# Feed-forward up-projections as seven Strassen block products, in groups of three row tiles, in a hybrid encoder block

## The chip, the cores and the metric

The kernel runs on one core of a Trainium2 chip. The time is device microseconds of one execution of the whole block; the profile is one execution recorded by the hardware profiler. PE is the matrix engine, PEld its weight load, DVE the vector engine, ACT the scalar engine, POOL GpSimd, and SP the engine that issues most DMAs.

## The reference

One layer of an encoder block for a sequence of 1024 with 1024 channels, in float32:

```python
h = rms_norm(x, norm_mix_g)
proj = h @ w_in                               # MLA, RWKV-7 and gate columns
o_a = mla_branch(...)                         # latent attention, 8 heads
o_b = rwkv7_branch(...)                       # forward and backward recurrence
x = x + (sig(gA) * (o_a @ w_o[:512]) + sig(gB) * (o_b @ w_o[512:])) @ w_merge
h = rms_norm(x, norm_ffn_g)
gp = dwconv_centered(h @ w_ffn_gate, ffn_conv_w, ffn_conv_b)   # three taps along the sequence
x = x + (silu(gp) * (h @ w_ffn_up)) @ w_ffn_down               # hidden width 2816
```

## The kernel before

Everything is held transposed: channels on the partitions, the 1024 positions along the free axis, so that a product makes one row tile of 128 output channels by 1024 positions, as two halves of 512 (`HT`), each in its own PSUM bank.

**Products.** A float32 operand is carried as the sum of two fp32r tiles, and a product is three passes: weight high part by operand high and low part, weight low part by operand high part (`mmk`, lines 248, 249 and 251). A step of 128 rows of depth is six matmuls of 128x512. The operands in x are split once and stay in SBUF; each weight block of 128x512 (four steps) is loaded by a DMA of SP's, and `split` (lines 163 and 164) makes its parts: ACT copies the high part (`whi`), POOL subtracts it (`wlo`). `product` runs the steps of a whole row tile.

**Phases.** A and B are the projection, the attention and the recurrence; the order of PE's instructions there is worked out by the kernel's own generators. Phase C makes the branches' second part, the merge (`w_merge`, eight row tiles into `x2`) and, after each row tile of the merge, the feed-forward part's operand: `h2h` and `h2l` (the residual times the norm's gain, split) in the places of `hp`, a pool on the right side of SBUF. The sum of squares for 1/rms gathers in `acc`; `rs2` (1/rms) multiplies the products when they leave PSUM.

**Phase D** is the feed-forward part. It goes over 22 row tiles f of the hidden width, in four groups (6, 6, 5, 5). For each f the gate product (8 steps) and the up product (8 steps) use 96 matmuls. The gate product leaves PSUM as `u` (L1517), is convolved (ACT L1522, DVE L1523 and L1524), goes through Silu (L121) and times rs2 (POOL, L1527), then is multiplied by the up product (L1528), and the result is split into `sh` and `sl`. After a group, eight down products over its tiles are added to `x2` (L1535); after the last group each row tile of x2 is stored.

**Order.** PE's instructions run in the order in which the code emits them (`manual_schedule`), each engine's queue in order. The order of DVE, ACT, POOL and SP is set by the framework's scheduler, from its own estimates. PSUM in phase D is four double banks in turn (`big4`).

Of the kernel before, what the change touches and what calls it, by code (L numbers as in the profile page):

```python
# [10 lines left out]
F32 = mybir.dt.float32  # L11
R = mybir.dt.float32r
# [17 lines left out]
GROUPS = ((0, 6), (6, 12), (12, 17), (17, 22))  # L30
# [18 lines left out]
# How long a step of phase B takes to be ready after it has left TensorE's queue, in ns  # L49
# [39 lines left out]
def block_kernel(ctx: ExitStack, tc: tile.TileContext, a):  # L89
# [539 lines left out]
    def gate_done(j):  # L629
        def done(ps):  # L630
            for x, hs in zip(ps, HT):
                gt = wpool["g"].tile([128, 512], F32, tag="gt", name="gt")
                V.tensor_tensor(out=gt, in0=x, in1=rstd[:, hs], op=mult)
                (G if j >= 14 else nc.sync).dma_start(d_gate[j][:, hs], gt)
# [996 lines left out]
```

## Time and profile before

| | |
|---|---|
| time, median of 3 runs | 2131.5 us (2128.46 to 2133.38) |
| span of the profiled execution | 2126.6 us |
| time of that execution itself | not listed apart; the span lies 4.9 us below the median of the runs |
| PE busy | 1958.1 us (92%), 12280 matmuls |
| DVE, ACT, POOL busy | 997.4, 843.1, 871.8 us |
| HBM traffic | 151.20 MB read, 63.60 MB written, 101 GB/s over the span |
| phase D | from 1394 us to the end |

In the profile's rows a group or an instruction is named by its line, engine, operation and tiles (out<-in); behind it stand busy or own time and the idle time of its engine just before, with what ended that. The granted clock is that of PE, as a share of full speed.

### The profile page before, as it was taken

How to read it: one execution, taken by the hardware profiler on the slowest of the kernel's cores; microseconds unless marked ns; L12 is line 12 of the kernel's file. 1: busy time of each engine (PE TensorE's matmuls, PEld its weight loads, DVE VectorE, ACT ScalarE, POOL GpSimd, SP SyncE). 2: the span in 40 equal slices, each digit the busy share in tenths (PEclk: the TensorE clock that was granted, in tenths of full speed). 3: DMA queues.
4: the chain of work that ended last, by engine and by line, in shares of the span. 5: the costliest groups of instructions: out<-in, count | busy, mean ns of one | idle time of the engine just before them, and what ended most of it. 6: DMA issues, size and time to landing. Idle time of an engine off the chain costs nothing.

```text
span 2126.6 us, 31745 instructions
## 1 busy us (share of the span) xinstructions
PE 1958.1 (92%) x12280; PEld 1507.2 (71%) x12280; DVE 997.4 (47%) x1560; ACT 843.1 (40%) x1459; POOL 871.8 (41%) x763
## 2 busy tenths in 40 slices
PE   7799999899898779888779999999999999999999
PEld 5566667677666556556557678888888888888887
DVE  8566766626474768667773235232212321221321
ACT  4676564123233546565547644232212211221221
POOL 7344546133233646564546432433323322332331
PEclk9899999899998989999989999999999999999999
DMA  3047447354344334352433685111111111111113
GB/s 144 34 140 230 145 162 219 104 145 113 98 130 125 78 108 106 104 135 79 100 86 91 205 303 189 50 45 50 43 53 50 50 43 52 50 39 56 50 38 117
DMA packets 212551, 221.09 MB, mean 104 GB/s; under 512 B 114152, under 2 KB 138792, under 8 KB 212400
## 3 DMA queue, kind: packets, MB, share of 16 engines
q1 hardware_dynamic: 212080, 218.01, 33.4%
q8 instruction: 97, 1.59, 0.3%
q0 software_dynamic: 320, 1.05, 0.1%
q14 instruction: 54, 0.44, 0.1%
HBM read 151.20 MB, written 63.60 MB: 101 GB/s over the span
## 4 chain that ended last, share of the span: by engine, by line
PE 51%; DVE 7%; DMA 3%; issue 1%; SPq 1%; POOL 0%; ACT 0%; DVEq 0%; POOLq 0%; ACTq 0%
PE b L251 13%; PE b L248 13%; PE b L249 13%; DMA IN<-dn 2%; DVE Ti L815 2%; DVE tm L811 2%; DVE mx L1151 1%; PE po L1179 1%; PE st L1205 1%; PE po L1181 1%; PE st L1207 1%; PE po L1180 1%; PE st L1206 1%; PE ct L972 1%; PE st L248 1%
## 5 line engine op out<-in xcount | busy, mean ns | idle before, releaser
L164 POOL TENSOR_TENSOR wlo<-wraw,whi 128x512 fp32r<-128x512 f32 x248 | 306.8, 1240 | 792.6 <-ACT whi L163 788.7
L163 ACT CAST whi<-wraw 128x512 fp32r<-128x512 f32 x248 | 145.2, 586 | 652.4 <-PE b L249 462.1
L248 PE MATMUL b<-h2h,whi 128*128 128x512 f32 x704 | 274.3, 390 | 0.0
L249 PE MATMUL b<-h2l,whi 128*128 128x512 f32 x704 | 273.9, 389 | 0.0
L1217 POOL TENSOR_TENSOR pl<-pe,ph 128x512 fp32r<-128x512 f32 x128 | 169.6, 1327 | 131.2 <-ACT ph L1216 128.6
L251 PE MATMUL b<-h2h,wlo 128*128 128x512 f32 x704 | 216.7, 389 | 0.0
L248 PE MATMUL st<-hh,whi 128*128 128x512 f32 x408 | 176.0, 431 | 15.2 <-ACT hh L275 9.0
L249 PE MATMUL st<-hl,whi 128*128 128x512 f32 x408 | 164.7, 404 | 0.5 <-DVE hl L276 0.5
L248 PEld LDWEIGHTS b<-h2h,whi 128*128 128x128 f32 x704 | 132.2, 188 | 27.7 <-issue 0.2
L249 PEld LDWEIGHTS b<-h2l,whi 128*128 128x128 f32 x704 | 132.2, 188 | 27.7 <-issue 0.2
L251 PEld LDWEIGHTS b<-h2h,wlo 128*128 128x128 f32 x704 | 132.2, 188 | 27.5
L251 PE MATMUL st<-hh,wlo 128*128 128x512 f32 x408 | 140.9, 400 | 0.5 <-POOL wlo L164 0.5
L248 PE MATMUL b<-sh,whi 128*128 128x512 f32 x352 | 138.8, 394 | 0.0
L249 PE MATMUL b<-sl,whi 128*128 128x512 f32 x352 | 138.7, 394 | 0.0
L1535 DVE TENSOR_TENSOR x<-b,x 128x1024 f32<-128x1024 f32 x32 | 39.2, 1225 | 197.6 <-PE b L251 197.6
L811 DVE TENSOR_TENSOR tm<-IN,Ti 128x126 f32<-128x126 f32 (+22 forms) x248 | 91.2, 368 | 77.5 <-DMA IN<-dn 71.3
L251 PE MATMUL b<-sh,wlo 128*128 128x512 f32 x352 | 110.4, 394 | 0.0
L248 PEld LDWEIGHTS st<-hh,whi 128*128 128x128 f32 x408 | 79.6, 195 | 43.0 <-issue 9.8
L815 DVE TENSOR_TENSOR Ti<-Ti,tm 128x126 f32<-128x126 f32 (+22 forms) x248 | 104.3, 421 | 6.6
L1517 DVE TENSOR_TENSOR u<-b,rs 128x1024 f32<-128x1024 f32 x22 | 26.9, 1224 | 169.6 <-PE b L251 158.4
L1216 ACT CAST ph<-pe 128x512 fp32r<-128x512 f32 x128 | 79.1, 620 | 64.5 <-PE po L1181 61.3
L980 POOL TENSOR_TENSOR sm<-RR,pcs 64x128 f32<-64x128 f32 x112 | 47.6, 425 | 126.4 <-DVE RR L1002 105.2
(333 smaller groups left out, 4159.1 us busy)
## 6 DMA issues: line engine op xcount, KB each, us to landing
wraw<-w_in SPq DMA_DIRECT2D x64, 256.0 KB
wraw<-w_fg SPq DMA_DIRECT2D x44, 256.0 KB
wraw<-w_fu SPq DMA_DIRECT2D x44, 256.0 KB
ld<-d_x SPq DMA_DIRECT2D x32, 256.0 KB
wraw<-w_fd SPq DMA_DIRECT2D x32, 256.0 KB
d_gate<-gt SPq DMA_DIRECT2D x28, 256.0 KB
xt<-xT SPq DMA_DIRECT2D x8, 512.0 KB
d_s<-sg SPq DMA_DIRECT2D x8, 512.0 KB
```

Source lines behind the costliest of these rows:

```text
L163: S.copy(hi, x)
L164: (eng or G).tensor_tensor(out=lo, in0=x, in1=hi.bitcast(F32), op=sub)
L248: nc.tensor.matmul(o, wh, xh[:, hs], start=first, stop=False)
L249: nc.tensor.matmul(o, wh, xl[:, hs], start=False, stop=False)
L251: nc.tensor.matmul(o, wl, xh[:, hs], start=False, stop=last)
L811: t = V.tensor_tensor(out=tm[:, 0:nt, 0:nj], in0=IN[:, s, s + 1:32][:, :, None].to_broadcast([128, nt, nj]), in1=Ti[:, s, 0:nj][:, None, : ...
L815: V.tensor_tensor(out=Ti[:, s + 1:32, 0:nj], in0=Ti[:, s + 1:32, 0:nj], in1=tm[:, 0:nt, 0:nj], op=add)
L980: state["pool"] = G.tensor_tensor(out=sm[hs], in0=RR[hs, :, h, 0, :], in1=pcv[hs, i // 4, :, i % 4, None].to_broadcast([64, 2, C]), op=mult)
L1216: S.copy(ph, pe)
L1217: G.tensor_tensor(out=pl, in0=pe, in1=ph.bitcast(F32), op=sub)
L1517: V.tensor_tensor(out=u, in0=pg, in1=rs2, op=mult)
L1535: V.tensor_tensor(out=x2[:, j, :], in0=ps, in1=x2[:, j, :], op=add)
```

## The change

The two products of a tile f are one product of a 2x2 block matrix: up and gate rows of the weights (`w_fu`, `w_fg`), each in two halves of the depth (A11, A12 the up weights, A21, A22 the gate weights, 128x512 each), by the operand in two halves of the depth and two of the positions (B11, B12; B21, B22). Instead of eight block products it makes seven, by Strassen's scheme in Winograd's form, from sums of weights (s1 = A21+A22, s2 = s1-A11, A11-A21, A12-s2, on DVE) and of operand blocks (U1 to U4, made once). A block product is called a quarter and is 12 matmuls: four steps of three passes on one bank. In PE's order they are A11 by B11 (bank ba), s2 by U2 (bb), s1 by U1 (bc), A11-A21 by U3 (bb again), A12 by B21 (ba), A22 by U4 (bb), A12-s2 by B22 (bc). A bank that is used again goes on accumulating, so its next quarter waits until DVE or ACT has read what it held (p1, u2, u3, u[1]); the results are put together by DVE when they leave PSUM. So 84 matmuls a tile.

Beside that:

- The groups are eight: six of three tiles, two of two. The down products of a group are emitted after the third quarter of the next group's first tile; those of the last group at the end, the first three of them interleaved by step.
- Operand blocks: B11, U1, B21, B22 lie in hp, U2 and U3 in a new pool bq, U4 in phase D's pool fp. They are made in the merge's loop, U4 from U2 and x2 when phase D starts. An operand block is four pairs of 128x512.
- Weights: six raw tiles, three pairs of parts in turn (`parts_`). PSUM in phase D is eight single banks.
- The stores of the gate tiles 14 and 15 in phase A go from ACT's queue instead of POOL's, and the framework's scratch for dynamic DMAs is 1024 bytes.

The core of the diff (removed comments are left out):

```diff
-GROUPS = ((0, 6), (6, 12), (12, 17), (17, 22))
+GROUPS = ((0, 3), (3, 6), (6, 9), (9, 12), (12, 15), (15, 18), (18, 20), (20, 22))
...
-                (G if j >= 14 else nc.sync).dma_start(d_gate[j][:, hs], gt)
+                (S if j >= 14 else nc.sync).dma_start(d_gate[j][:, hs], gt)
...
+    def quarters(pairs):
+        return [tuple(p[k // 2][:, HT[k % 2]] for p in pairs) for k in range(4)]
+    def in_hp(i, n):
+        return quarters([[place(f"h{x}{i + q}", f"{n}{x}") for q in range(2)] for x in "hl"])
+    def in_pool(pl, n, i):
+        return quarters([[pl.tile([128, T], R, tag=f"b{i + 2 * c + q}", name=f"{n}{x}{q}") for q in range(2)] for c, x in enumerate("hl")])
+    B11, U1, B21, B22 = in_hp(0, "b11"), in_hp(2, "t1"), in_hp(4, "b21"), in_hp(6, "b22")
+    U2, U3 = in_pool(bq, "t2", 0), in_pool(bq, "t3", 4)
+    tq = y2.enter_context(pool("tq"))
     acc = place("rstd", "acc2", F32)
+    def scaled(dst, src, g):
+        S.activation(dst[0], src, AF.Copy, scale=g)
+        V.scalar_tensor_tensor(out=dst[1], in0=src, scalar=g, in1=dst[0].bitcast(F32), op0=mult, op1=sub)
     for j in range(8):
         ps, two_ = big4()
         for _ in product(two_, a["w_merge"][j], yx):
             pass
         V.tensor_tensor(out=x2[:, j, :], in0=ps, in1=x2[:, j, :], op=add)
-        h2x.append((place(f"hh{j}", "h2h"), place(f"hl{j}", "h2l")))
-        hh, hl = h2x[j]
-        S.activation(hh, x2[:, j, :], AF.Copy, scale=vc("gffn", j))
-        V.scalar_tensor_tensor(out=hl, in0=x2[:, j, :], scalar=vc("gffn", j), in1=hh.bitcast(F32), op0=mult, op1=sub)
+        k, g = j % 4, vc("gffn", j)
+        x1, x2_ = (x2[:, j, hs] for hs in HT)
+        if j < 4:
+            scaled(B11[k], x1, g)
+            d = tq.tile([128, 512], F32, tag="d", name="d")
+            G.tensor_tensor(out=d, in0=x2_, in1=x1, op=sub)
+            scaled(U1[k], d, g)
+        else:
+            g0, x10, x20 = vc("gffn", k), *(x2[:, k, hs] for hs in HT)
+            scaled(B21[k], x1, g)
+            scaled(B22[k], x2_, g)
+            d = tq.tile([128, 512], F32, tag="d", name="b12")
+            S.activation(d, x20, AF.Copy, scale=g0)
+            t3 = tq.tile([128, 512], F32, tag="t3", name="t3f")
+            V.scalar_tensor_tensor(out=t3, in0=x2_, scalar=g, in1=d, op0=mult, op1=sub)
+            split(t3, *U3[k], V)
+            t2 = tq.tile([128, 512], F32, tag="t2", name="t2f")
+            V.scalar_tensor_tensor(out=t2, in0=x10, scalar=g0, in1=t3, op0=mult, op1=add)
+            split(t2, *U2[k], V)
...
+    U4 = in_pool(fp, "t4", 0)
...
+    for k in range(4):
+        t = f5("up", 1)
+        V.scalar_tensor_tensor(out=t, in0=x2[:, 4 + k, HT[0]], scalar=vc("gffn", 4 + k), in1=U2[k][0].bitcast(F32), op0=mult, op1=sub)
+        V.tensor_tensor(out=t, in0=t, in1=U2[k][1].bitcast(F32), op=sub)
+        split(t, *U4[k], V)
+    nraw, nwt = [0], [0]
+    def raw_():
+        nraw[0] += 1
+        if nraw[0] % 6 == 0:
+            return wpool["g"].tile([128, 512], F32, tag="gt", name="ra")
+        return f5("ra", 5)
+    def parts_(x, n=512):
+        nwt[0] += 1
+        if nwt[0] % 3 == 0:
+            hi, lo = (fp.tile([128, 512], R, tag=t, name=t) for t in ("wh", "wl"))
+        else:
+            hi, lo = (wpool["w"].tile([128, 512], R, tag=t, name=t) for t in ("whi", "wlo"))
+        hi, lo = hi[:, 0:n], lo[:, 0:n]
+        split(x, hi, lo)
+        return hi, lo
+    def quarter(ps, w, xs, first):
+        for k, (xh, xl) in enumerate(xs):
+            ws = slice(k * 128, (k + 1) * 128)
+            for m, (wt, x) in enumerate(((w[0], xh), (w[0], xl), (w[1], xh))):
+                nc.tensor.matmul(ps, wt[:, ws], x, start=(first and k == 0 and m == 0), stop=(k == 3 and m == 2), skip_group_check=True)
+    sh, sl = {}, {}
+    def gate_up(f):
+        def load(w, h):
+            t = raw_()
+            nc.sync.dma_start(t, a[w][f][:, HT[h]])
+            return t
+        A11, A21, A22 = load("w_fu", 0), load("w_fg", 0), load("w_fg", 1)
+        s1, s2 = raw_(), raw_()
+        A12 = load("w_fu", 1)
+        ba, bb, bc = bank(), bank(), bank()
+        quarter(ba, parts_(A11), B11, True)
+        p1 = f5("p1")
+        S.copy(p1, ba)
+        V.tensor_tensor(out=s1, in0=A21, in1=A22, op=add)
+        V.tensor_tensor(out=s2, in0=s1, in1=A11, op=sub)
+        V.tensor_tensor(out=A21, in0=A11, in1=A21, op=sub)
+        quarter(bb, parts_(s2), U2, True)
+        u2 = f5("u2")
+        V.tensor_tensor(out=u2, in0=bb, in1=p1, op=add)
+        if f == 0:
+            for hs in HT:
+                ss = bank()
+                nc.tensor.matmul(ss, ones, acc[:, hs], start=True, stop=True)
+                rsqrt_(rs2[:, hs], ss, 1.0 / D, eps)
+        quarter(bc, parts_(s1), U1, True)
+        V.tensor_tensor(out=s2, in0=A12, in1=s2, op=sub)
+        yield
+        quarter(bb, parts_(A21), U3, False)
+        u3 = f5("u3")
+        V.tensor_tensor(out=u3, in0=bb, in1=p1, op=add)
+        quarter(ba, parts_(A12), B21, False)
+        u = fp.tile([128, T], F32, tag="u", name="u")
+        V.tensor_tensor(out=u[:, HT[1]], in0=bc, in1=u3, op=add)
+        quarter(bb, parts_(A22), U4, False)
+        V.tensor_tensor(out=u[:, HT[0]], in0=bb, in1=p1, op=add)
+        V.tensor_tensor(out=u, in0=u, in1=rs2, op=mult)
+        quarter(bc, parts_(s2), B22, False)
+        cv = fp.tile([128, T], F32, tag="cv", name="cv")
+        S.activation(cv, u, AF.Identity, scale=vc("cw1", f), bias=vc("cb", f))
+        V.scalar_tensor_tensor(out=cv[:, 1:], in0=u[:, :-1], scalar=vc("cw0", f), in1=cv[:, 1:], op0=mult, op1=add)
+        V.scalar_tensor_tensor(out=cv[:, :-1], in0=u[:, 1:], scalar=vc("cw2", f), in1=cv[:, :-1], op0=mult, op1=add)
+        act(cv, cv, AF.Silu)
+        G.tensor_tensor(out=cv, in0=cv, in1=rs2, op=mult)
+        up = f5("up")
+        V.tensor_tensor(out=cv[:, HT[0]], in0=ba, in1=cv[:, HT[0]], op=mult)
+        V.tensor_tensor(out=up, in0=bc, in1=u2, op=add)
+        V.tensor_tensor(out=cv[:, HT[1]], in0=up, in1=cv[:, HT[1]], op=mult)
+        sh[f], sl[f] = (fp.tile([128, T], R, tag=t, name=t, bufs=3) for t in ("sh", "sl"))
+        split(cv, sh[f], sl[f], V)
+        yield
+    def down(f0, f1, last):
+        n = f1 - f0
+        def weights(j):
+            t = wpool["w"].tile([128, n * 128], F32, tag="wraw", name="wraw")
+            nc.sync.dma_start(t, a["w_fd"][j, :, f0 * 128:f1 * 128])
+            return parts_(t, n * 128)
+        def mm(two_, w, k):
+            ws = slice(k * 128, (k + 1) * 128)
+            mmk(two_, w[0][:, ws], w[1][:, ws], (sh[f0 + k], sl[f0 + k]), k == 0, k == n - 1)
+        def out(j, two_):
+            for o, hs in zip(two_, HT):
+                V.tensor_tensor(out=x2[:, j, hs], in0=o, in1=x2[:, j, hs], op=add)
+            if last:
+                nc.sync.dma_start(a["outT"][j * 128:(j + 1) * 128, :], x2[:, j, :])
+        j0 = 0
+        if last:
+            j0 = 3
+            js = [([bank(), bank()], weights(j)) for j in range(3)]
+            for k in range(n):
+                for two_, w in js:
+                    mm(two_, w, k)
+            for j, (two_, _) in enumerate(js):
+                out(j, two_)
+        for j in range(j0, 8):
+            two_, w = [bank(), bank()], weights(j)
+            for k in range(n):
+                mm(two_, w, k)
+            out(j, two_)
...
     for gi, (f0, f1) in enumerate(GROUPS):
         for f in range(f0, f1):
+            part = gate_up(f)
+            next(part)
+            if f == f0 and gi:
+                down(*GROUPS[gi - 1], False)
+            next(part)
+    down(*GROUPS[-1], True)
```

How it moves instructions. DVE in phase D, one tile before (the gate product's way out of PSUM to the split result):

```order
L1517 TENSOR_TENSOR u_13872<-b_13811,rs_12751 128x1024
L1523 SCALAR_TENSOR_TENSOR cv<-u_13872,vec,cv 128x1023
L1524 SCALAR_TENSOR_TENSOR cv<-u_13872,vec,cv 128x1023
L1528 TENSOR_TENSOR sg_13939<-b_13874,sg_13939 128x1024
L164 TENSOR_TENSOR sl<-sg_13939,sh 128x1024
```

DVE after, inside a group, from the taps of one tile on (ra is a raw weight tile or a sum of two, p the copy of p1, bank a PSUM bank; u_14138 is u2 and u_14173 is u3 of the tile that follows):

```order
L1617 SCALAR_TENSOR_TENSOR cv<-u,vec,cv 128x1023
L1618 SCALAR_TENSOR_TENSOR cv<-u,vec,cv 128x1023
L1596 TENSOR_TENSOR u_14138<-bank,p_14117 128x512
L1622 TENSOR_TENSOR cv<-bank,cv 128x512
L1624 TENSOR_TENSOR cv<-up,cv 128x512
L164 TENSOR_TENSOR sl<-cv,sh 128x1024
L1591 TENSOR_TENSOR ra<-ra 128x512
L1607 TENSOR_TENSOR u_14173<-bank,p_14117 128x512
L1593 TENSOR_TENSOR ra<-ra 128x512
L1610 TENSOR_TENSOR u<-bank,u_14173 128x512
L1592 TENSOR_TENSOR ra<-ra 128x512
L1612 TENSOR_TENSOR u<-bank,p_14117 128x512
```

The additions u2 and u3 of a tile now stand between the last steps of the tile before it, and u3 stands behind that tile's sl and behind the first weight sum (L1591) of the tile after.

ACT at the step from the merge into phase D, before (the last two row tiles of the merge, each with the two weight casts of a product ahead of time, then the first function of 1/rms):

```order
L163 CAST whi<-wraw 128x512 x2
L1488 ACTIVATE h2h<-x_12750,vec 128x1024
L1493 ACTIVATE rs_12751<-x_12750 128x1024
L163 CAST whi<-wraw 128x512 x2
L121 ACTIVATE rs_12751<-b_13731,cst 128x1024
```

ACT there after (the last row tile of the merge, the high parts of its operand blocks, then the first casts of phase D):

```order
L1497 ACTIVATE b21h<-x_12750,vec 128x512
L1497 ACTIVATE b22h<-x_12750,vec 128x512
L1527 ACTIVATE rs_12751<-x_12750 128x1024
L163 CAST t3h_13138<-t3f 128x512
L163 CAST t2h_13134<-t2f 128x512
L163 CAST t4h_13746<-up 128x512
L163 CAST whi<-ra 128x512
```

The first weight casts of phase D stood two products ahead; now the first of them (whi from ra) stands behind the operand blocks of the last merge row tile and behind the first high part of U4 (t4h).

DVE at the same place after, from the last addition into x2 on (b21l, b22l, t3l, t2l are low parts, up is the temporary of U4):

```order
L1504 TENSOR_TENSOR x_12750<-b_13658,x_12750 128x1024
L1519 SCALAR_TENSOR_TENSOR t3f<-x_12750,vec,b_13724 128x512
L1498 SCALAR_TENSOR_TENSOR b21l<-x_12750,vec,b21h 128x512
L1522 SCALAR_TENSOR_TENSOR t2f<-x_12750,vec,t3f 128x512
L1498 SCALAR_TENSOR_TENSOR b22l<-x_12750,vec,b22h 128x512
L164 TENSOR_TENSOR t3l_13140<-t3f,t3h_13138 128x512
L164 TENSOR_TENSOR t2l_13136<-t2f,t2h_13134 128x512
L1546 SCALAR_TENSOR_TENSOR up<-x_12750,vec,t2h_13133 128x512
L1547 TENSOR_TENSOR up<-up,t2l_13135 128x512
L164 TENSOR_TENSOR t4l_13748<-up,t4h_13746 128x512
```

Eight operations stand between that addition and the tile from which t4h is cast.

More of the change, by code (lines that the diff above doesn't have):

```diff
@@ L1450, in block_kernel @@
     rs2 = xp2.tile([128, T], F32, name="rs2")
-    y2, tl = ExitStack(), ExitStack()
+    bq = ctx.enter_context(pool("bq"))
+    y2 = ExitStack()
     yq = y2.enter_context(pool("yq"))
     yx = [(yq.tile([128, T], R, name=f"yh{j}"), yq.tile([128, T], R, name=f"yl{j}")) for j in range(8)]
-    yp = tl.enter_context(pool("yp"))
-    psc = [ctx.enter_context(psum("psc", 2))]
+    psc = [y2.enter_context(psum("psc", 2))]
     nps = [0]
@@ L1465, in block_kernel @@
         if j == 2:
-            psc.append(ctx.enter_context(psum("psc1", 2, "right")))
-        y0 = yp.tile([128, T], F32, tag="y0", name="y0", bufs=2)
+            psc.append(y2.enter_context(psum("psc1", 2, "right")))
+        y0 = bq.tile([128, T], F32, tag=f"b{j % 2}", name="y0")
         nc.sync.dma_start(y0, d_y0[j])
-        y = yp.tile([128, T], F32, tag="gt", name="gt", bufs=2)
+        y = bq.tile([128, T], F32, tag=f"b{2 + j % 2}", name="gt")
         for _ in branch(1, j, xs, big4()[1], y):
@@ L1498, in block_kernel, with bank, f5 @@
     fp = ctx.enter_context(pool("fp"))
-    ones = fp.tile([128, 128], F32, name="ones")
-    G.memset(ones, 1.0)
-    sh = fp.tile([128, 6, T], R, name="sh")
-    sl = fp.tile([128, 6, T], R, name="sl")
-    def ft(n, tag):
-        return fp.tile([128, T], F32, tag=tag, name=n, bufs=2)
+    pd = ctx.enter_context(psum("pd", 8))
+    U4 = in_pool(fp, "t4", 0)
+    def bank():
+        return pd.tile([128, 512], F32, tag="bank", name="bank")
+    def f5(n, bufs=1):
+        return fp.tile([128, 512], F32, tag=n, name=n, bufs=bufs)
@@ L1507, in block_kernel @@
     for gi, (f0, f1) in enumerate(GROUPS):
         for f in range(f0, f1):
-            pg, two_ = big4()
-            for _ in product(two_, a["w_fg"][f], h2x):
-                pass
-            if f == 0:
-                ss = big4()[0]
-                mm32(ss, ones, acc)
-                rsqrt_(rs2, ss, 1.0 / D, eps)
-            u = ft("u2", "f2")
-            V.tensor_tensor(out=u, in0=pg, in1=rs2, op=mult)
-            pu, two_ = big4()
-            for _ in product(two_, a["w_fu"][f], h2x):
-                pass
@@ L1521, in block_kernel @@
-            cv = ft("cv", "f0")
-            S.activation(cv, u, AF.Identity, scale=vc("cw1", f), bias=vc("cb", f))
-            V.scalar_tensor_tensor(out=cv[:, 1:], in0=u[:, :-1], scalar=vc("cw0", f), in1=cv[:, 1:], op0=mult, op1=add)
-            V.scalar_tensor_tensor(out=cv[:, :-1], in0=u[:, 1:], scalar=vc("cw2", f), in1=cv[:, :-1], op0=mult, op1=add)
-            sg = ft("sg2", "f1")
-            act(sg, cv, AF.Silu)
-            G.tensor_tensor(out=sg, in0=sg, in1=rs2, op=mult)
-            V.tensor_tensor(out=sg, in0=pu, in1=sg, op=mult)
@@ L1529, in block_kernel @@
-            split(sg, sh[:, f - f0, :], sl[:, f - f0, :], V)
-        n = f1 - f0
-        for j in range(8):
-            ps, two_ = big4()
-            for _ in product(two_, a["w_fd"][j, :, f0 * 128:f1 * 128], [(sh[:, k, :], sl[:, k, :]) for k in range(n)]):
-                pass
-            V.tensor_tensor(out=x2[:, j, :], in0=ps, in1=x2[:, j, :], op=add)
-            if gi == len(GROUPS) - 1:
-                nc.sync.dma_start(a["outT"][j * 128:(j + 1) * 128, :], x2[:, j, :])
+            part = gate_up(f)
```

5 lines of the change are left out of this document (2 added, 3 removed).

## The prediction

> **What bounds the kernel now.** I read the page first, then the feed-forward stage, where the change works, in windows and by groups of instructions, and last single instructions there. The page (second block: busy tenths in 40 slices of the span):
>
> ```profile
> span 2126.6 us, 31745 instructions
> PE 1958.1 (92%) x12280; PEld 1507.2 (71%) x12280; DVE 997.4 (47%) x1560; ACT 843.1 (40%) x1459; POOL 871.8 (41%) x763
> PE   7799999899898779888779999999999999999999
> PEclk9899999899998989999989999999999999999999
> ```
>
> TensorE is busy in nine tenths or more of every slice from about 1117 us on (21 slices of 53.2), through the last branch products, the merge and the feed-forward part. Three windows of it (span, busy us of PE, PEld, DVE, ACT, POOL, granted clock, DMA share, GB/s):
>
> ```profile
> 1390.00:1450.00 60.00, 60.00 (x262) 48.83 (x262) 15.90 (x12) 18.38 (x21) 21.01 (x15) 1.00 0.15 49
> 1600.00:1700.00 100.00, 100.00 (x443) 82.81 (x442) 28.76 (x23) 26.43 (x32) 34.82 (x24) 1.00 0.15 48
> 1700.00:1800.00 100.00, 100.00 (x435) 80.99 (x434) 18.49 (x15) 16.24 (x26) 27.63 (x24) 1.00 0.16 48
> ```
>
> There PE never waits, at full clock, while DVE, ACT and POOL are at 35% or less and DMA is at 0.16. The first of them holds the step from the merge into the feed-forward part, which costs nothing today. A matmul taken out is therefore worth its whole length, as long as nothing else becomes late.
>
> **What a matmul costs there.** Starts of two instructions five row tiles apart, and of two matmuls of the last down products ten steps of six matmuls apart, and what stands last (from the timeline and the chain):
>
> ```profile
> 1604.88 1.22 DVE L1517 TENSOR_TENSOR u<-b,rs 128x1024 f32<-128x1024 f32 x1 [9.68 <-PE b L251]
> 1713.68 1.22 DVE L1517 TENSOR_TENSOR u<-b,rs 128x1024 f32<-128x1024 f32 x1 [7.24 <-PE b L251]
> 2090.10 0.47 PE b L251 x2
> 2104.10 0.47 PE b L251 x2
> 2121.43 1.22 DVE x L1535
> ```
>
> Five tiles take 108.80 us, so one takes 21.76 us for 96 matmuls: 0.2267 each, with the moving operand in the hp tiles. The down products take 14.00/60 = 0.2333 each, with the operand in the other pool. After the change a tile has 84: four quarters (B11, U1, B21, B22) from hp, 48 x 0.2267 = 10.88, and three (U2, U3, U4) from the other side, 36 x 0.2333 = 8.40; together 19.28. **Saving: 2.48 x 22 = 54.6 us**; 47.5 if all take 0.2333, 59.8 if all take 0.2267. That the pool is the reason for the two figures is an inference, so both ends stay. The down products do the same work as before.
>
> **What it adds elsewhere.** Groups of the stage (busy, mean ns, idle before them), and a DVE group of phase A for the 128x512 size:
>
> ```profile
> L164 POOL TENSOR_TENSOR wlo<-wraw,whi 128x512 fp32r<-128x512 f32 x108 | 139.8, 1294 | 430.0 <-ACT whi L163 429.9
> L163 ACT CAST whi<-wraw 128x512 fp32r<-128x512 f32 x108 | 67.1, 621 | 415.6 <-PE b L249 353.9 <-issue 61.7
> L1527 POOL TENSOR_TENSOR sg<-sg,rs 128x1024 f32<-128x1024 f32 x20 | 47.9, 2396 | 0.0
> L1524 DVE SCALAR_TENSOR_TENSOR cv<-u,vec,cv 128x1023 f32<-128x1023 f32 x20 | 25.7, 1285 | 0.7
> L1522 ACT ACTIVATE cv<-u,vec 128x1024 f32<-128x1024 f32 x20 | 24.9, 1246 | 20.9 <-DVE u L1517 20.9
> L164 DVE TENSOR_TENSOR sl<-sg,sh 128x1024 fp32r<-128x1024 f32 x20 | 24.5, 1225 | 22.3 <-ACT sh L163 22.3
> L121 ACT ACTIVATE sg<-cv 128x1024 f32<-128x1024 f32 x20 | 21.1, 1057 | 0.0
> L163 ACT CAST sh<-sg 128x1024 fp32r<-128x1024 f32 x20 | 21.0, 1049 | 23.4 <-DVE sg L1528 23.4
> L633 DVE TENSOR_TENSOR gt<-st,rstd 128x512 f32<-128x512 f32 x20 | 13.8, 689 | 24.0 <-PE st L251 17.9 <-DMA d_gate<-gt 5.8
> ```
>
> Per tile POOL then has seven weight splits and the product with rs2: 7 x 1.294 + 2.396 = 11.45 us (7.57 now). ACT has three casts and the copy of p1 more, about 4 x 0.62; it stays under half busy. DVE gets four weight sums and five additions with PSUM at about 0.69 each. What matters is whom DVE meets:
>
> ```profile
> 900.55 0.28 DVE L815 TENSOR_TENSOR Ti<-Ti,tm 128x126 f32<-128x126 f32 x1
> 910.44 1.28 POOL L1187 TENSOR_TENSOR pc<-pc 64x512 f32<-64x512 f32 x1 [0.61 <-ACT pc L121]
> 910.50 1.33 DVE L815 TENSOR_TENSOR Ti<-Ti,tm 128x96 f32<-128x96 f32 x1
> 1412.84 1.51 POOL L164 TENSOR_TENSOR wlo<-wraw,whi 128x512 fp32r<-128x512 f32 x1 [5.94 <-ACT whi L163]
> 1413.24 2.19 DVE L1524 SCALAR_TENSOR_TENSOR cv<-u,vec,cv 128x1023 f32<-128x1023 f32 x1
> 902.48 1.27 POOL L1217 TENSOR_TENSOR pl<-pe,ph 128x512 fp32r<-128x512 f32 x1 [1.83 <-ACT ph L1216]
> 902.59 0.69 DVE L1151 TENSOR_REDUCE mx<-st 128x1 f32<-128x512 f32 x1
> ```
>
> A DVE operation of 0.28 us took 1.33 when it began just after a POOL operation, and ended 0.11 us after it; the 1.285 us one at 1413.24 took 2.19 and ended 1.08 us after POOL's. L1151, which reads PSUM, kept its 0.69 beside POOL. So a DVE operation with two SBUF inputs and a POOL operation run one after the other. Those of a tile after the change: four sums 2.76, u x rs2 1.22, two taps 2.57, one half of cv 0.69, sl 1.22, together 8.5 us; with POOL's 11.45 that is 19.9 us in 19.28 us of PE's time (11.4 in 21.76 now). Only the down products between groups give relief.
>
> **Where it reaches PE.** (1) *Entry.* The first split weight (A11) stands on ACT behind the first t4h, and that behind DVE's work on the last merge product: x2 addition 1.22, then eight operations of 128x512 (t3f, b21l, t2f, b22l, t3l, t2l, two for t4) 8 x 0.69 = 5.5, t4h 0.62, the cast 0.62, POOL's subtraction 1.29: 9.3 with nothing between. PE has nothing else queued. POOL's last acc addition (2.4) and handovers raise it to 13 at most 16; I take **+13**, since six of those operations have two SBUF inputs.
> (2) *End.* From q6's end: u[0] 0.69, u x rs2 1.22, Identity 1.25, taps 2.57, Silu 1.06, POOL 2.40, two halves 1.38, sh 1.05, sl 1.22 = 12.8, with ten handovers of 0.05 13.3, less q7's 2.8: sl is there 10.5 us after q7. Only three interleaved products' first tile (18 matmuls, 4.2 us) covers it: **+6.5** (4 to 9). Now the fifth tile's chain is covered by the first four.
> (3) *Seven changes of group.* The down products of a group start after three quarters (8.24 us) of the next tile and need the third tile's sl two steps (2.8) later, at 11.04 after its q7. The chain of (2) is 10.5 without port waits. Five of its operations use the port; three splits in 11 us make POOL busy 35% of it, some 0.4 us each: 1.5 late, six times, and 2.9 for the two-tile group: **+12** (0 to 25).
> (4) *Inside a group.* q6 writes the bank that u3 (L1607) reads, one quarter after q4. On DVE u3 stands behind the tile before's taps, halves, sl, and the next tile's first weight sum (L1591): 10.5 + 0.69 + 0.69 = 11.9 after the last q7; q6 is due after five quarters, 13.76. Slack 1.9. Six operations there use the port, POOL busy 59%: a wait of 0.38 on average if they fall anywhere in a split, 0.76 if always at its start; 0.55 in between gives 3.3 - 1.9 = 1.4 us for the 14 tiles that follow another in their group: **+20** (6 to 37).
> (5) *Clock.* Rows of a PE gap and the window after it, twice:
>
> ```profile
> 1269.78 0.50 PE L248 MATMUL b<-o,whi 128*128 128x512 f32 x1 [2.54 <-ACT whi L163]
> 1267.00:1270.00 3.00, 0.46 (x3) 1.00 0.94 365
> 1272.00:1275.00 3.00, 3.00 (x8) 0.50 0.92 339
> 1275.00:1280.00 5.00, 5.00 (x23) 0.98 0.87 342
> 1128.49 0.89 PE L997 MATMUL ct<-RR,BT 128*64 128x64 f32 x8 [1.65 <-DVE RR L985]
> 1130.00:1132.50 2.50, 2.50 (x15) 0.64 0.32 125
> ```
>
> After 2.54 us of idleness PE ran at 0.50 for about 3.4 us, after 1.65 us at 0.64 in the window that follows: 1.7 us lost by the first. The gaps (1) and (2) cost two such: **+3.3**. For the waits of (3) and (4) I take none, as they lie below the smaller gap shown; up to 1.7 each is rival two.
> (6) *The rest.* Four gate stores leave POOL's queue for ACT's:
>
> ```profile
> L634 POOL DMA_DIRECT2D d_gate<-gt x4 | 2.4, 604 | 12.8 <-DVE gt L633 11.9 <-DVE RR L985 0.9
> ```
>
> POOL is rid of 2.4 us and ACT has to issue four, in phase A/B, where a wait ends now on one engine, now on another: 0, between -4 and +4. The new blocks B21, t2, t3 in the merge have 11.2 us of PE (48 matmuls at 0.2333) per row tile to hide in and some 5.5 of DVE, 3.1 to 3.7 of ACT. Twice as many x2 additions go to idle DVE, 0.69 us against a down product of 4.2. The w_fd loads move up SP's queue between raw weights; DMA is at 0.16. Nothing for these.
>
> **Sum**: -54.6 + 13 + 6.5 + 12 + 20 + 3.3 + 0 = +0.2 us on the profiled execution of 2126.6 us span. The runs' median is 2131.5, 4.9 above that span, which holds launch and end; I add the sum to the median: 2132 us.
>
> **Rivals.** *One, the port is hidden* (faster). If DVE's operations mostly fall beside POOL's pauses, (4) stays in its slack of 1.9 us and (3) at 2: -54.6 + 11 + 6.5 + 2 + 0 + 3.3 = -32, **2100 us**. For it: the taps average 1285 ns over 20 tiles, so meetings are rare at 11.4 of 21.76 us. Against: 19.9 of 19.28 leaves no pauses.
> *Two, half clock after the small waits* (slower). If waits of 1.4 us set PE to half clock as 1.65 did, 21 places cost up to 1.7, half of them 18 us: **2150 us**. It decides from some 12 such places on. For: the row at 1128.49. Against: it mixes small matmuls with its gap, and most of the waits may be below 1 us. The Trainium skill (TensorE: Matmul & The Clock Gate, Part 1: The HAM clock gate) has PE throttled after at least one idle window of about 3.4 us and asks only for no longer gaps; by it rival two would not exist and the sum would stay at 2132, but the 2.54 us gap above was followed by 0.50, so I keep it.
> *Three, the pitch*: 47.5 saved gives 2139, 59.8 gives 2127.
> *Four*: a reordering of A/B by its stores, +-4.
>
> **How the numbers follow.** About 0.2% (4.3 us) is what a measurement of this kernel can tell from no change. The forecast with its own range (2120 to 2145, pitch included) 0.50: faster 0.12, same 0.20, slower 0.18. Rival one 0.24, nearly all faster. Rival two 0.20, nearly all slower. What is left, 0.06, is split. Faster 0.37, same 0.24, slower 0.39. The range runs from rival one's 2100 to rival two's 2150 and 1 more.
>
> **What would show it.** Right: tiles of 19.3 us plus 1 to 2; PE idle in front of q6 with DVE L1607 as releaser, at about 1.4 us on 14 tiles; 13 us before the first quarter, released by POOL's wlo; 6.5 us in the last 30 us; taps (L1617, L1618) over 1.285 and POOL's splits over 1.294 us on average; a clock of 1.00 except after the first and last gap. Wrong: no idle PE in the tiles (rival one), PEclk digits below 9 throughout the stage (rival two), a tile period far above 21.8 us (a bound I have not seen, such as POOL at its full 11.45 us plus blocked time), or a changed time before 1267 us.

## The result, and the profile after

The changed kernel takes 2143.18 us (median of 5 runs, 2140.81 to 2151.77), the kernel before 2131.5 (5 runs, 2124.63 to 2134.46): ratio 1.0062, 95% interval 1.004 to 1.0084. It is slower by 0.6%: inside the range of the prediction, but 11 us above its 2132 us, and the interval leaves "no change" out. The profiled execution takes 2141.4 us, its span is 2139.5. The page of after:

```profile
span 2139.5 us, 31989 instructions
PE 1924.6 (90%) x12016; PEld 1463.6 (68%) x12016; DVE 1279.7 (60%) x1912; ACT 900.6 (42%) x1573; POOL 1013.6 (47%) x829
PE   7799999899897789788879989989999999999997
PEclk9899999999999889899889999989999999999999
```

The changed kernel has 264 matmuls fewer and PE's busy time is 33 us shorter, yet the span is 13 us longer. DVE has 282 us more to do, POOL 142. PE's waits from 1300 us on (total, times, longest, in us), where the kernel before has none:

```profile
PE bank L1573 <- DVE u L1607: 19.6, 13, 2.7
PE bank L1573 <- ACT whi L163: 10.1, 1, 10.1
PE bank L248 <- ACT sh L163: 8.9, 8, 5.6
PE bank L249 <- DVE sl L164: 5.8, 8, 0.8
```

Two more waits come to 0.6 us. These are the predicted places: u3 (L1607) in the groups' second and third tiles, A11's cast at the entry, sh and sl at eight starts of down products, the last of these (5.58 and 0.46 us) at the end. The entry's wait ends with ACT's cast, not with POOL's subtraction as the prediction had it. It reads in the timeline:

```profile
1399.89 1.23 DVE L1504 TENSOR_TENSOR x<-b,x 128x1024 f32<-128x1024 f32 x1 [3.69 <-PE b L251]
1403.51 2.67 POOL L1528 TENSOR_TENSOR acc<-acc,rs 128x1024 f32<-128x1024 f32 x1 [8.46 <-ACT rs L1527]
1403.97 2.76 DVE L164 TENSOR_TENSOR t3l<-t3f,t3h 128x512 fp32r<-128x512 f32 x1
1408.81 0.62 ACT L163 CAST t4h<-up 128x512 fp32r<-128x512 f32 x1 [4.35 <-DVE up L1547]
1410.00 0.79 PE L1573 MATMUL bank<-b11h,whi 128*128 128x512 f32 x1 [10.15 <-ACT whi L163]
```

The whole chain is there: x2, DVE's operations with t3l held for 2.76 us beside POOL's accumulation, t4h, and right behind it the cast. The port (a DVE operation with two SBUF inputs and a POOL operation that reads SBUF run one after the other) shows in the tiles as longer operations on both engines. Groups between 1400 and 2105 us:

```profile
L164 POOL TENSOR_TENSOR wlo<-ra,whi 128x512 fp32r<-128x512 f32 x103 | 159.7, 1556 | 150.0 <-ACT whi L163 149.4 <-POOL wlo L164 0.6
L1618 DVE SCALAR_TENSOR_TENSOR cv<-u,vec,cv 128x1023 f32<-128x1023 f32 x21 | 46.2, 2199 | 0.8
L1613 DVE TENSOR_TENSOR u<-u,rs 128x1024 f32<-128x1024 f32 x22 | 44.7, 2032 | 0.7
L1591 DVE TENSOR_TENSOR ra<-ra 128x512 f32<-128x512 f32 x22 | 30.4, 1381 | 6.3 <-POOL wl L164 3.6 <-POOL wlo L164 2.7
```

Their lengths before were 1.294 us (POOL), 1.285, 1.224 (with u still in PSUM) and, for 128x512, 0.689. Last, the granted clock in windows of 20 us (span, PE busy, clock, DMA share, GB/s):

```profile
1400.00:1420.00 20.00, 9.87 (x27) 0.66 0.11 36
1440.00:1460.00 20.00, 16.91 (x66) 0.91 0.17 52
2040.00:2060.00 20.00, 17.74 (x70) 0.91 0.15 47
2100.00:2120.00 20.00, 13.96 (x48) 0.83 0.12 38
```

It falls in these four windows of the part and in no other; busy time times what is missing from 1.00 is 3.4 + 1.5 + 1.6 + 2.4 = 8.9 us.

### The profile page after: what moved, and what is told of

The parts are those of the page before. It is cut to its first block, busy times and chain, and to the rows that moved or that the text cites. A ratio compares the mean times of both kernels' runs of the same rounds, so it can differ in the third digit from the quotient of the medians.

```text
span 2139.5 us, 31989 instructions
## 1 busy us (share of the span) xinstructions
PE 1924.6 (90%) x12016; PEld 1463.6 (68%) x12016; DVE 1279.7 (60%) x1912; ACT 900.6 (42%) x1573; POOL 1013.6 (47%) x829
## 3 DMA queue, kind: packets, MB, share of 16 engines
q1 hardware_dynamic: 212080, 218.01, 33.6%
## 4 chain that ended last, share of the span: by engine, by line
PE 38%; DVE 17%; DMA 6%; POOL 6%; issue 5%; ACT 2%; SPq 1%; DVEq 0%; POOLq 0%; ACTq 0%
PE bank L1573 6%; PE bank L249 4%; PE bank L251 4%; PE bank L248 3%; DMA IN<-dn 3%; DVE Ti L815 3%; DVE tm L811 3%; POOL cv L1620 2%; POOL wlo L164 2%; PE b L251 2%; PE b L248 2%; PE b L249 2%; DVE u L1613 2%; DVE mx L1151 2%; DVE ra L1591 1%
## 5 line engine op out<-in xcount | busy, mean ns | idle before, releaser
L164 POOL TENSOR_TENSOR wlo<-wraw,whi 128x512 fp32r<-128x512 f32 (+2 forms) x139 | 180.6, 1301 | 382.2 <-ACT whi L163 362.0
L164 POOL TENSOR_TENSOR wlo<-ra,whi 128x512 fp32r<-128x512 f32 x103 | 159.7, 1556 | 150.0 <-ACT whi L163 149.4
L163 ACT CAST whi<-wraw 128x512 fp32r<-128x512 f32 (+2 forms) x139 | 80.2, 577 | 232.3 <-PE bank L249 86.8
L1643 DVE TENSOR_TENSOR x<-bank,x 128x512 f32<-128x512 f32 x128 | 82.5, 686 | 153.3 <-PE bank L251 153.3
L164 POOL TENSOR_TENSOR wl<-ra,wh 128x512 fp32r<-128x512 f32 x51 | 80.3, 1575 | 74.5 <-ACT wh L163 74.5
L248 PE MATMUL bank<-sh,whi 128*128 128x512 f32 x236 | 95.8, 406 | 6.7 <-ACT sh L163 6.7
L249 PE MATMUL bank<-sl,whi 128*128 128x512 f32 x236 | 94.8, 402 | 3.5 <-DVE sl L164 3.5
L121 ACT ACTIVATE pe<-st 128x512 f32<-128x512 f32 x128 | 76.2, 596 | 41.3 <-PE st L1207 33.5
L251 PEld LDWEIGHTS st<-hh,wlo 128*128 128x128 f32 x408 | 78.7, 193 | 20.4 <-POOL wlo L164 2.4
L1151 DVE TENSOR_REDUCE mx<-st 128x1 f32<-128x512 f32 x112 | 73.3, 683 | 31.0 <-PE st L1150 30.7
L249 PEld LDWEIGHTS st<-hl,whi 128*128 128x128 f32 x408 | 79.7, 195 | 16.9 <-DVE hl L276 1.6
```

Of the source, the lines that this page charges most:

```text
L163: S.copy(hi, x)
L164: (eng or G).tensor_tensor(out=lo, in0=x, in1=hi.bitcast(F32), op=sub)
L248: nc.tensor.matmul(o, wh, xh[:, hs], start=first, stop=False)
L249: nc.tensor.matmul(o, wh, xl[:, hs], start=False, stop=False)
L251: nc.tensor.matmul(o, wl, xh[:, hs], start=False, stop=last)
L1151: V.tensor_reduce(out=mx2[:, qt, i2:i2 + 1], in_=ps, axis=AX_X, op=ALU.max)
```

## The experiments

Each run is told with its ratio to the kernel before and the interval; the changed kernel's is 1.0062. The runs of the kernel before beside them have medians of 2129.0 and 2129.7 us; the ratios are against these.

Where x2's last addition in the merge starts differs between executions of the same code ahead of it: at 1389.1 and 1394.4 us in the two profiles with that code as it was before (before, and the run on the sides), at 1398.9 to 1414.3 us in the five with the changed kernel's (after, and the runs on the port, the order, the end and the change of group). So an edit behind that point is also told by the length of the feed-forward part, from that start to the end of the span: 732.2 us in before, 739.6 in the changed kernel, and 736.8 and 738.3 in the two runs that leave the changed part as it is.

**The port.** POOL's subtraction gives way to an operation that only writes.

```diff
-        split(x, hi, lo)
+        S.copy(hi, x)
+        G.memset(lo.bitcast(F32), 0.0)
```

> The changed kernel, with one thing left out: in the feed-forward part the weights' low part isn't subtracted by POOL but set to zero (a POOL operation that writes only), so the third pass of each product multiplies zeros. All matmuls, casts, weight sums and transfers stay. Theory 'port' (DVE's operations with two SBUF inputs stand still while POOL reads SBUF, which makes u3 late): L1618 falls from 2.20 to about 1.29 us, L1613 from 2.03 to 1.22, the first weight sum from 1.38 to 0.69, 2.4 us together, more than the 1.4 us by which u3 is late. So the 19.6 us of waits for u3 fall below 3, the waits for sh and sl at the group changes (8.7 us without the last) to about 0, and with the restarts and clock they cost the time falls by 30 to 36 us, to about 2110 (0.990 of before). Rival 'order' (u3 is late because it stands behind sl and the next weight sum, whatever POOL does): waits stay above 12 us, time 2130 to 2143.

Measured 2112.77 us, ratio 0.9902 (0.9869 to 0.9934); the part takes 708.9 us, 30.7 less. Its second tap (the group that had 2.199 us), and its waits:

```profile
L1619 DVE SCALAR_TENSOR_TENSOR cv<-u,vec,cv 128x1023 f32<-128x1023 f32 x22 | 28.3, 1285 | 0.8
```

```profile
PE bank L1574 <- ACT whi L1565: 10.1, 1, 10.1
PE bank L248 <- ACT sh L163: 6.3, 2, 5.1
PE bank L249 <- DVE sl L164: 5.8, 8, 0.8
```

The tap is back at its own length, as are the other operations of that chain, and no wait for u3 is left though u3 stands where it stood in DVE's order. So the port makes u3 late. Of PE's 45.0 us of waits 22.2 are left. The short waits for sl stay, against the expectation; they fit the 1.2 us from sh to sl, less the two matmuls that need only sh. POOL was also less busy here (a write takes 0.49 us), so the run doesn't part blocking from POOL's own length; the lengths of DVE's operations do.

**The order on DVE.** u3 goes ahead of the next tile's first weight sum.

```diff
+        i = V.tensor_tensor(out=s1, in0=A21, in1=A22, op=add)
+        if f:
+            tc.add_manual_dep(i.ins, u3s[f - 1].ins.name, NOSYNC, reason="after u3 of the tile before")
```

> The changed kernel, with the next tile's first weight sum (s1) put behind u3 in DVE's order, nothing else. Theory (u3 is late at the end of one chain, and DVE and POOL have time left elsewhere): u3 comes 1.38 us earlier, the 13 waits of 1.2 to 2.7 us fall to about 0.1 each, and with 0.23 us of restart each and the clock lost behind the longest the time falls by 20 to 24 us, to about 2121 (0.995 of before). Rival 'port full' (DVE and POOL together have no time left in a tile, 19.9 of 19.4 us): the delayed sum makes the second quarter's weights of the next tile late instead, PE waits there for the weight's low part by about as much, and the time stays within 5 us of 2143.

Measured 2137.99 us, ratio 1.0034 (1.0012 to 1.0056): in the median a fourth of what was expected. The profiled execution is the fastest of the twelve; its part takes 728.9 us, 10.7 less, half of what was expected. Its waits:

```profile
PE bank L248 <- ACT sh L163: 12.6, 8, 5.6
PE bank L1573 <- ACT whi L163: 11.2, 3, 10.1
PE bank L1573 <- DVE u L1609: 3.8, 5, 1.1
```

The waits for u3 fell by 15.8 us as expected, but sh came 3.7 us later in all and two waits for casts appeared (1.1): with another order DVE meets POOL elsewhere in the same chain (the first tap went from 1.31 to 1.67 us, u x rs2 from 2.03 to 1.53). Neither theory is whole.

**The end.** The down products of the group (18, 20) move behind the last quarter of tile 21.

```diff
+        if f == 21:
+            sh[f], sl[f] = (bq.tile([128, T], R, tag=t, name=n) for t, n in (("b0", "sh"), ("b1", "sl")))
...
-            if f == f0 and gi:
+            if f == f0 and gi and gi < 7:
...
+    down(*GROUPS[-2], False)
     down(*GROUPS[-1], True)
```

> The changed kernel, with the down products of the group (18, 20) put behind the last quarter of tile 21, so that 22.4 us of PE work lie between the last tile's chain and the last down products; sh and sl of tile 21 lie in the place of U2. Expected: the last wait (5.58 for sh, 0.46 for sl) and the half clock behind it (2.9 us) go, and so do the 2.26 us of waits at the start of that group's down products with the 1.9 us of clock behind them; tile 20 now follows tile 19 directly and gets a wait for u3 of about 1.6 us. Together -11 us, to about 2132. Rival (the end is bound by the stores and the last additions): no change from the last wait, at most -4.

Measured 2133.16 us, ratio 1.0007 (0.9988 to 1.0026), 10 us less than the changed kernel; the part takes 727.9 us, 11.7 less. Waits of this run:

```profile
PE bank L1573 <- DVE u L1607: 21.0, 14, 2.7
PE bank L249 <- DVE sl L164: 4.6, 6, 0.8
PE bank L248 <- ACT sh L163: 1.8, 6, 0.4
```

The long wait is gone, and tile 20 has its wait for u3, both as expected.

**The change of group.** Down products one quarter later.

```diff
-        yield
         quarter(bb, parts_(A21), U3, False)
         u3 = f5("u3")
         V.tensor_tensor(out=u3, in0=bb, in1=p1, op=add)
+        yield
```

> The changed kernel, with the down products of a group put behind the fourth quarter of the next group's first tile instead of the third. sh and sl of the group's last tile are due 2.8 us later. Theory (the waits there are the length of the chain from the last quarter to sl, 11.0 + about 1 us): the waits for sh and sl at seven group changes, 8.7 us, and the clock lost at the last of them, 1.9, go; those for u3 stay at 19 to 20 us; time -9 to -11, about 2133. Rival (POOL and DVE are so loaded there that the chain just moves with it): under -4.

Measured 2131.64 us, ratio 0.9997 (0.9976 to 1.0018), 11.5 us less than the changed kernel. The profiled execution is the slowest of the twelve (2140.07 us): x2's last addition starts only at 1414.27 there. Its part takes 724.0 us, 15.6 less. Its waits:

```profile
PE bank L1573 <- DVE u L1606: 19.9, 13, 2.7
PE bank L248 <- ACT sh L163: 5.6, 1, 5.6
PE bank L249 <- DVE sl L164: 0.5, 1, 0.5
```

Of the waits for sh and sl only the end's are left. In the median this one line takes back the whole loss. The part fell by more than the 8.6 us of waits that went and the clock lost at the last of them; the rest is not assigned.

**The entry.** The first tile's weights are prepared during the last merge product, its quarters go in another order, and U2's last block is made first on DVE (core of the diff).

```diff
+        p = parts_(A11)
+        i = V.tensor_tensor(out=s1, in0=A21, in1=A22, op=add)
+        q = parts_(s1)
+        V.tensor_tensor(out=s2, in0=s1, in1=A11, op=sub)
+        r = parts_(s2)
...
+    first0 = gate0()
+    make_u4(0)
+    residual(7, ps)
...
+        if not f:
+            quarter(bc, ws1, U1, True)
```

> The changed kernel with another entry into the feed-forward part: the first tile's weights A11, s1 and s2 are summed and split while the last merge product runs, its quarters run in the order A11, s1, s2, and on DVE the last block of U2 goes ahead of B21, B22, U3 and U4. Theory (the 10.15 us of idle PE are the chain x2 addition, eight operations on DVE, t4h, the cast, with the accumulation's 2.7 us on POOL in the middle): the first two quarters (5.5 us) start at once, the third waits about 1 us for U2, and the half clock behind the gap (3.9 us) goes too: -11 to -13 us, about 2131. Rival (the operands of the last merge row tile are needed anyway, so the wait only moves to the second or third quarter): -4 or less.

Measured 2138.75 us, ratio 1.0041 (1.0026 to 1.0057), -4.4 us; the part takes 734.0 us, 5.6 less. The rival was right:

```profile
PE bank L1614 <- ACT t4h L163: 7.5, 1, 7.5
PE bank L1614 <- DVE x L1505: 2.1, 1, 2.1
```

9.6 us of 10.15 are still waited: 2.1 for x2's PSUM bank and 7.5 ahead of the fourth quarter, where u2 stands on DVE behind U4's blocks. What is missing is DVE's time for the blocks: DVE has no pause over 0.7 us between 1398 and 1422 us.

**Ahead of the merge.** In the changed kernel x2's last addition in the merge starts later (1394.44 us before, 1399.89 after), where the prediction expected no change. First, y0's loads behind w_o on SP's queue.

```diff
-        nc.sync.dma_start(y0, d_y0[j])
...
+        i = nc.sync.dma_start(y0, d_y0[j])
+        tc.add_manual_dep(i.ins, wpool["load"].ins.name, NOSYNC, reason="after the branch's weights")
```

> The changed kernel with one order on SP's queue changed: in the branch products of phase C the load of y0 goes behind the branch's weights (w_o) instead of ahead. In the changed kernel two y0 loads of 512 KB stand ahead of the first w_o loads, PE waits 5.25 us for these (2.54 before) and then runs its first matmuls at half clock. Theory (that is a cost of the change, in phase C): the wait goes back to about 2.5 us, the merge ends 3 to 5 us earlier, time -4, about 2139. Rival (the later start of the feed-forward part is the spread between executions of the phases before): the wait stays near 5 us or the time stays within 2 us.

Measured 2142.8 us, ratio 1.0059 (1.0038 to 1.0079), and a wait of 5.4 us. It tells nothing on the theory, because the edit missed: the loads that PE waits for are those of row tiles 2 and 3, and y0 still went ahead of these, as SP's queue in this run shows:

```profile
1260.45 0.38 SPq L1471 DMA_DIRECT2D y<-d_y  x1
1263.38 0.47 SPq L1471 DMA_DIRECT2D y<-d_y  x1
1265.85 2.82 SPq L171 DMA_DIRECT2D wraw<-w_o  x2
```

Then the two other edits alone, on the kernel before.

```diff
-                (G if j >= 14 else nc.sync).dma_start(d_gate[j][:, hs], gt)
+                (S if j >= 14 else nc.sync).dma_start(d_gate[j][:, hs], gt)
...
+    nc = bacc.Bacc("TRN2", target_bir_lowering=False, num_devices=1, dynamic_dma_scratch_size=1024)
```

> The kernel before, with the two edits of the change that lie ahead of the merge and aren't Strassen's: the four gate stores go from ACT's queue instead of POOL's, and the scratch for dynamic DMAs is 1024 bytes. In eight profiles of changed kernels the last merge addition starts at 1399 to 1404 us, in two of kernels like before at 1389 and 1394; 5 us of it have come up by 1090 us. Theory (these two edits make phases A and B longer): +4 to +6 us, about 2135, the merge's end at 1396 to 1400. Rival (the spread between executions, or the new places of y0 and the gate in phase C alone): within 2 us of before.

Measured 2134.84 us, ratio 1.0021 (1.0006 to 1.0036): some 4.5 us (1.3 to 7.7). Its part takes 731.8 us, as before's 732.2, so they lie ahead of it. By the medians that is a third of the loss, by the interval between a tenth and three fifths, and it was never Strassen's. Which of the two edits it is, and by what wait, this run doesn't part. (The expectation's 1399 to 1404 us overlooks the 1414.27 in the profile of the change of group.) Then both additions undone on the changed kernel:

```diff
-                (S if j >= 14 else nc.sync).dma_start(d_gate[j][:, hs], gt)
+                (G if j >= 14 else nc.sync).dma_start(d_gate[j][:, hs], gt)
...
+        if j >= 2:
+            mixed(j - 2)
```

> The changed kernel, with both of its additions ahead of the merge undone: gate stores on POOL's queue again, and in phase C the y0 loads of row tile j behind the weights w_o of row tile j + 2 (the scratch stays at 1024 bytes, Strassen's part as it is). Theory: phases A and B come back by 5 us, the wait of about 5 us for w_o in phase C by 2.5 to 3.5 with its clock: -8 to -9 us, about 2134, 1.002 of before. If only the wait in phase C comes back: -3 to -4. Rival (spread): within 2 us of 2143.

Measured 2139.88 us, ratio 1.0051 (1.0028 to 1.0073): -3.3 us, not told from the changed kernel by the intervals. The same instruction in before, the run before this one, this one:

```profile
1394.44 1.22 DVE L1485 TENSOR_TENSOR x<-b,x 128x1024 f32<-128x1024 f32 x1 [7.47 <-PE b L251]
1397.84 1.22 DVE L1485 TENSOR_TENSOR x<-b,x 128x1024 f32<-128x1024 f32 x1 [7.47 <-PE b L251]
1395.91 1.23 DVE L1513 TENSOR_TENSOR x<-b,x 128x1024 f32<-128x1024 f32 x1 [3.67 <-PE b L251]
```

The start lies 4.0 us ahead of after's, well within the 15 us by which the five profiles named above differ, so it doesn't show that the edits did it. PE still waits 5.1 us for w_o's casts, most of it now at another place. The wait in phase C was not shown to be y0's.

**The sides.** On the kernel before, only the place of the down products' weight parts changes.

```diff
+                wh, wl = (fp.tile([128, m], R, tag=t, name=t, bufs=2) for t in ("dhi", "dlo"))
+                split(raw, wh, wl)
```

> The kernel before, with one thing moved: the split weight parts of the down products lie in phase D's pool on the left side of SBUF, where sh and sl lie, instead of the pool on the right. Theory 'same side' (a matmul of 128x512 takes 0.2267 us when its weights and its moving operand lie on the same side, 0.2333 when not): a step of six falls from 1.40 to 1.36 us, 176 steps, -7 us, about 2124. Rival 'place of the moving operand' (the left pool is slower whatever the weights): no change of the step. Rival 'content': the pitch belongs to what sh holds: no change.

Measured 2122.68 us, ratio 0.9972 (0.9956 to 0.9988), -6 us; the part takes 725.1 us, 7.1 less than before's, as expected. Two matmuls ten steps apart:

```profile
2061.03 0.45 PE b L251 x2
2074.63 0.45 PE b L251 x2
```

13.60 us where before took 14.00. So the left pool as such isn't slow: the longer pitch goes with weights and moving operand in pools on different sides. The changed kernel shows the same within one tile (first matmuls of four quarters):

```profile
1462.55 0.39 PE L1573 MATMUL bank<-t2h,whi 128*128 128x512 f32 x1
1465.35 0.39 PE L1573 MATMUL bank<-t1h,whi 128*128 128x512 f32 x1
1468.09 0.39 PE L1573 MATMUL bank<-t3h,wh 128*128 128x512 f32 x1
1470.82 0.39 PE L1573 MATMUL bank<-b21h,whi 128*128 128x512 f32 x1
1474.98 0.47 PE L1573 MATMUL bank<-t4h,whi 128*128 128x512 f32 x1 [1.24 <-DVE u L1607]
```

U2 (left) with whi (right) takes 2.80 us; U1 (right) with whi 2.74, U3 (left) with wh (left) 2.73. The other way round, B22 (right) with wh (left), from 1477.86 to 1480.66 us, it is 2.80 again.

**All together.** u3 first, the entry, the end, the down products later, and the y0 edit (which, as told, does nothing).

> All edits together on the changed kernel: u3 ahead of the next weight sum, the new entry, the last two groups' down products behind the last quarter, the other groups' behind the fourth quarter, y0 behind w_o. If the waits are independent: -5 (u3 first, as measured), -12 (entry), -10 (end, as measured), -8 (group changes, without the part that the end has already), -4 (y0): about 2104, 0.987 of before. If one wait takes the place of another (the port between DVE and POOL stays full in the tiles), the group tiles show waits for u3 or the weights' low parts of over 10 us in all, and the time is above 2112.

Measured 2102.59 us, ratio 0.9877 (0.9859 to 0.9896), 40.6 us less than the changed kernel and 26 less than before. Its waits:

```profile
PE bank L1615 <- ACT t4h L163: 5.9, 1, 5.9
PE bank L1615 <- DVE u L1659: 4.7, 7, 0.8
PE b L248 <- ACT whi L163: 4.2, 1, 4.2
PE bank L1615 <- DVE x L1506: 2.1, 1, 2.1
```

The sum came out, though entry and y0 gave less than their terms. By the parts it fits better: the four edits alone shortened theirs by 10.7, 5.6, 11.7 and 15.6 us, 43.6 together (some 4 us, the last change of group, stand in two of them), and all together it is 696.2 us, 43.4 less. Last, with gate stores on POOL, y0 later, weights on their operand's side, and a third order of the first tile's quarters:

```diff
+        if left:
+            hi, lo = (fp.tile([128, 512], R, tag=t, name=t, bufs=2) for t in ("wh", "wl"))
+        else:
+            hi, lo = (wpool["w"].tile([128, 512], R, tag=t, name=t) for t in ("whi", "wlo"))
```

> The version with all edits together (2102.6 us), and in addition: gate stores on POOL's queue and y0 behind w_o as in the run beside this one (-8), the weights that meet U2, U3, U4, sh or sl in pairs on the left side and the others on the right, so that weights and moving operand always share a side (a quarter of 2.72 us instead of 2.80 in some 3 of 7 quarters, -5; a down step of 1.36 instead of 1.40 in two thirds of them, -5), and at the start of the feed-forward part A12 by B21 ahead of (A11-A21) by U3 and the last three blocks of U4 behind u2 on DVE (-3 to -5). Together about 2081, 0.977 of before. Rival (two pairs of weights on a side instead of three for both leave too little time for the split): waits for the weights' low parts of over 10 us, and the time above 2095.

Measured 2098.87 us, ratio 0.9857 (0.9834 to 0.988): the fastest version here, but 18 us above the expectation and not told from the last one by the intervals. Most quarters did become 2.71 to 2.77 us. But the part takes 698.6 us, no less than the 696.2 with all together: what the quarters gave went into waits for u3 again. Why u3 is late here was not tried:

```profile
PE bank L1622 <- DVE u L1669: 16.9, 9, 5.0
PE b L248 <- ACT whi L163: 6.7, 2, 4.3
```

## Why the prediction was right or wrong

By its own steps, from x2's last merge addition to the end of the span (739.6 us after, 732.2 before: +7.4):

| step | predicted | measured |
|---|---|---|
| saving | -54.6 (47.5 to 59.8) | about -52.8: clean tiles 19.36 us on average |
| (1) entry | 13 | 10.15 |
| (2) end | 6.5 | 6.0 |
| (3) changes of group | 12 | 8.7 (sh 3.3, sl 5.3) |
| (4) u3 | 20, 14 waits | 19.6, 13 waits |
| (5) clock | 3.3 | 8.9 in this execution |
| restart after a wait | none | 3: 13 times some 0.23 |
| (6) A to C | 0 (-4 to +4) | +5.5 in these two executions |

The table's measured terms of the part come to +4 us (with 0.6 of small waits); 3 of its 7.4 stay unassigned, most of them in the down products, 34.9 us a group with the waits where 33.6 and 1.0 were expected.

**Right**: the mechanism and the places. The saving given back by the port, entry, end and group changes was the likeliest case, each at the row named, and the first run showed that the port is the cause inside the tiles. The Trainium skill (SBUF — State Buffer, SBUF: two separate sides) states that the lock lies between a DVE operation with two SBUF inputs and a GpSimd operation that reads SBUF; a POOL operation that only writes left DVE at 1.285 us here, against 2.20, which agrees.

**Wrong, the sign**: "about no change" was 0.6% slower. Two steps failed. One is (6): the gate stores were costed at 0 because POOL is rid of 2.4 us, and the scratch had no term; the two alone cost about 4.5 us. The table's +5.5 is one pair out of a spread, but all five profiles with the changed kernel's code ahead of the part start it later than both with the code as it was. By what wait is open. The other is (5): only two gaps were counted. The 2.73 us wait for u3 at 1452 us and the 1.50 and 0.76 us at 2049 also brought the half clock, and the end's gap lost 2.4.

**Luck**: inside the part, (1) and (3) came out 6.2 us smaller than forecast, which hides that the clock cost 5.6 more. PE's first matmul needs only the high part of its weight, so POOL's 1.29 us in (1) was not in that path.

Three readings were off without moving the sum: there are 19 slices from 1117 us on, not 21; all eight operations at the entry have two SBUF inputs, not six; and the 4.9 us between span and median are not launch and end, as an execution's time lies only 1.9 us above its span (2141.4 and 2139.5).

**Rival two** did not come: after single waits of 1.24 to 1.51 us the windows keep 1.00. For longer waits, length alone does not decide. In the last version the windows around waits of 1.45, 2.12 and 1.53 us read:

```profile
1556.00:1564.00 8.00, 6.55 (x30) 1.00 0.09 32
1650.00:1658.00 8.00, 5.88 (x19) 0.79 0.11 33
1743.00:1751.00 8.00, 6.47 (x29) 1.00 0.08 24
```

After 2.12 us PE lost clock. Yet a wait of 3.06 us in the same version, ended at 1401.44, was followed by 1.00. So was the first of the waits for u3 in the run on the change of group, though the same wait cost the changed kernel clock (0.91 in the second of its windows above):

```profile
1467.05 0.47 PE L1573 MATMUL bank<-t4h,whi 128*128 128x512 f32 x1 [2.73 <-DVE u L1606]
1467.00:1475.00 8.00, 7.95 (x35) 1.00 0.09 33
```

So a part of (5) is chance. The rule of the Trainium skill quoted in the prediction (TensorE: Matmul & The Clock Gate, Part 1: The HAM clock gate) asks for gaps of no more than about 3.4 us; by the row at 1650 that doesn't always suffice.

**Rival three**, the pitch, was the wrong reading of a right pair of numbers: 0.2267 and 0.2333 belong to no pool but to the pair of places. **Rival one** comes nearer without POOL's subtractions: in the first run no wait for u3 was left, at 2112.8 us against its 2100.

## What to carry to other kernels

An algebraic saving on the busy engine is paid in additions on engines that had time, and what counts is not their sum but the chain from one tile's last product to the bank that the next tile needs: here 11.9 us without port waits, due after 13.8 (both the prediction's estimates from before's rows). Where two of those engines share a port, count their operations on it together and compare with the tile; then move the consumer (one `yield` line, one group's down products) rather than the producers. Side edits that make room for the main one are to be timed alone.

## What the runs showed of the hardware

- A 128x512 fp32r matmul took 0.2267 us with weights and moving operand in pools on the same side of SBUF and 0.2333 us on different sides, in both kernels and, in the changed one, both ways round; moving the weights alone gained 6 us (ratio 0.9972). Whether the side or something that goes with it, such as the address, is the cause was not tried.
- Whether a wait of PE is followed by some 3.4 us at half clock differs between executions of the same instructions. The first of the waits for u3 (2.71 to 2.75 us) was in two profiles (after, the end) and not in three (change of group, y0, both additions undone); the 1.65 us of the prediction's row at 1128.49 was in five of the thirteen profiles. From 1240 us on every wait of 4.2 us or more was, and no single one of 1.54 us or less in the tiles. Two waits in a row can count together: 1.50 and 0.76 us with two matmuls between were followed by it in after, and not in the run on y0.
- A wait of some 1.3 us costs about 0.2 us beside itself: the quarter before it took 2.92 us (4.16 less the wait of 1.24, in the rows above) and the one after it 2.88, against 2.76 and 2.80 without a wait. Most of the 0.16 before it is how the trace counts: idle time begins at the end of the last matmul (0.39 us), while the next one otherwise starts 0.23 us after it.
